# Moving the start columns of operand buffers for TensorE in a two-layer encoder trunk

## The chip, the cores and the metric

The kernel runs on one core of a Trainium2 chip. The metric is the device time of one execution in microseconds (us); of several executions the median counts. TensorE does the matrix products, ScalarE (ACT in the profile) and VectorE (DVE) prepare operands and drain results, and the queues of SyncE (SP) and GpSimd (POOL) issue most DMA transfers.

A matmul on TensorE has two operands in the on-chip memory. The **stationary** one, 128x128, is loaded into the array by an instruction of its own (LDWEIGHTS, row PEld of the profile). The **moving** one, here 256, 272 or 512 columns wide, streams past it (MATMUL, row PE). A float32 column is 4 bytes in each of the 128 partitions. "Column" below always means a place of 4 bytes along a partition.

## The reference

Two layers over 512 tokens of width 1024. Each is a token mixer and a gated feed-forward block, both with RMSNorm and a residual. What the change touches are two products: the `v` part of the second layer's mixer, and the second layer's last down projection.

```python
def gla_mixer(h, w_g2, b_g, norm_g):          # layer 1; h = rmsnorm(x) @ gla_w_in
    q, k, v, r, gl = jnp.split(h, [...], axis=-1)
    g = jax.nn.log_sigmoid((gl @ w_g2 + b_g).astype(f32)) / GLA_TAU
    ...                                        # chunked gated linear attention over q, k, v, g
    return o                                   # normed, times silu(r)

def conv_ffn(h, w_up, conv_w, conv_b, w_down):
    u, v = jnp.split(h @ w_up, 2, axis=-1)
    u = causal_dwconv(u, conv_w, conv_b)
    return (jax.nn.gelu(u, approximate=False) * v) @ w_down

for l in range(2):
    x = x + mixer(rmsnorm(x, mix_norm[l]))     # layer 0: pooling and short convolution; layer 1: GLA
    x = x + conv_ffn(rmsnorm(x, ffn_norm[l]), ...)
return rmsnorm(x, final_norm)
```

## The kernel before

Every product is done in three passes: each float32 operand is split into a high part (a copy rounded to the type float32r, made by ACT) and a low part (the rest, made by DVE), and high x high, high x low and low x high are added up in one accumulator. So each block of weights that DMA brings into a `raw` buffer is turned into a `hi` and a `lo` buffer before TensorE may use it: `high()` and `low()` inside `fetch_steps` (L260 and L264) for plain blocks, L531 and L537 inside `seven_weights` for the large products, which are done as seven half-size products (L650).

**Who is stationary.** In all large products the weights are stationary, in blocks of 128 columns, and activations move. In the `v` product it is the other way round: `v_chunk` (L1535 to L1537) has 128 tokens of `xh` or `xl` stationary and lets 256 or 272 columns of the weights `hi` or `lo` move. `v` has four column groups (272, 256, 256, 256 wide; the first holds 16 columns for the low-rank gate) and 8 rows of 128 in depth. A buffer takes 3, 3 and 2 depth rows of the wide group, or 4 and 4 of a narrow one. For each depth row and each of four token tiles there are three matmuls, so a buffer gives 36, 36, 24, or 48 matmuls: 96 with 272 columns and 288 with 256.

**Where operands begin.** The `hi` and `lo` buffers are 1088 columns long (`WPITCH`), which is 17 times 64, and hold up to 1024. Weights of the seven-product form begin 19 columns in (`SKEW`), those of `v` 48 columns in (`VG_SKEW`), those of plain blocks at 0. The last down tile is done in halves of 256 tokens. Its two weight blocks are used twice, so they are kept in two buffers of their own (`kept_block` in `last_pair`, L1028), which hold the 5 high blocks and 3 of the 5 low ones, from column 0; the other two low blocks go to a plain slot called `rest`. Per half and block there are 15 matmuls, 13 with a stationary operand in `kept` and 2 in `rest`: 60 in all.

The addresses in the built program show that the stationary tiles `xh` and `xl`, all activation slots and all weight buffers begin at the same place of a period of 64 columns. For a matmul, the column at which its moving operand begins less the one at which its stationary operand begins, modulo 64, is thus set by these offsets alone:

| matmuls | before | after |
|---|---|---|
| seven-product form (activation at 0, weights 19 in) | 45 | 45 |
| `v`, 256 wide (weights 48 in, then every 256) | 48 | 45 |
| `v`, 272 wide (depth rows 1, 2, 3 of a buffer) | 48, 0, 16 | 45, 45, 45 |
| last down tile, `kept` | 0 | 45 |
| last down tile, `rest` | 0 | 0 |

**What sets the order.** A planner in the kernel gives each step a due time (`at`, `then`, `block`), sorts the steps, and writes each engine's program in that order (`run_plan`). In the `v` stage each buffer's load, high and low step stand some 13, 8 and 6.6 us of planned time ahead of its use (`next_block`). Each finished column group is drained by ACT (`v_out`, L1542) and DVE (`v_low`, L1552). The first attention pair follows it. `seven_weights` also loads a tile `s31` from the pool's tag `sum`, the same tag as the kept buffers in the stage `dn`.

Of the kernel before, what the change touches and what calls it, by code (L numbers as in the profile page):

```python
# [7 lines left out]
F32 = mybir.dt.float32  # L8
F32R = mybir.dt.float32r
# [5 lines left out]
P = 128  # L15
# [16 lines left out]
WBLK = 1024  # L32
WPITCH = WBLK + 64
SKEW = 19
VG_SKEW = 48
NBIG = 48
NSIDE = 8
AHEAD = 1
# [74 lines left out]
def trunk_kernel(ctx, tc, xT, cols, w_first, w_lead, w_ab, w_pool, w_abo, w_abp, w_vg, w_qk, w_r, w_g2, w_go, w_up, w_dn, w_ds, w_de, out):  # L113
# [6 lines left out]
    wsp = ctx.enter_context(tc.tile_pool(name="wsp", bufs=4))  # L120
# [4 lines left out]
    def slot(dt=F32, name="s"):  # L125
        return big.tile([P, T], dt, tag="s", name=name)

    stage = {}
# [84 lines left out]
    def f32(ap):  # L213
        return ap.bitcast(F32)
# [5 lines left out]
    def down_blocks():  # L220
        yield from ((j, k0, kt) for k0, kt in zip(DOWN_AT, DOWN_K) for j in range(4))
        yield from ((j, k0, kt) for j in range(4, KD) for k0, kt in zip(DOWN_AT, DOWN_K))

    def weight_order():
        for j in range(4):
            for b in (4 + j, 8 + j, j):
                yield w_ab[b], KD, P
        for j in ABO:
            if not isinstance(j, tuple):
                yield w_abo[j], KD, P  # L230
        for l in range(2):
            for j, k0, kt in down_blocks():
                yield w_dn[l, j, :, k0 * P : (k0 + kt) * P], kt, P, SKEW * (l == 1 and j == KD - 1)
            if l == 0:
                off = 0
                for n, ks in zip(VG_COLS, VG_K):
                    for kt in ks:
                        yield w_vg[:, off : off + kt * n], kt, n, VG_SKEW
                        off += kt * n
                for j in TILE_ORDER:  # L240
                    yield w_go[j], KD, P
# [3 lines left out]
    ready = []  # L245
# [3 lines left out]
    def fetch_steps():  # L249
        src, kt, n, *skew = next(order)  # L250
        fetched[0] += 1
        m = kt * n
        h0 = skew[0] if skew else 0
        raw = wp.tile([P, WBLK], F32, tag="raw", name="raw")[:, :m]
        loads.append(nc.sync.dma_start(raw, src).ins)
        parts = []

        def high():
            parts.append(wsp.tile([P, WPITCH], F32R, tag="hi", name="hi")[:, h0 : h0 + m])
            S.activation(parts[0], raw, AF.Copy)  # L260

        def low():
            parts.append(wsp.tile([P, WPITCH], F32R, tag="lo", name="lo")[:, h0 : h0 + m])
            V.tensor_tensor(parts[1], raw, f32(parts[0]), ALU.subtract)  # L264
            ready.append([t.rearrange("p (k n) -> p k n", k=kt) for t in parts])

        return high, low

# [208 lines left out]
    def at(t, fn):  # L477
        events.append((t, len(events), fn))
# [24 lines left out]
    def seven_weights(src, base, pool, sums, behind=False, lead=None, later=0.0, begin=(26.0, 20.0, 15.4, 9.7), early=0.0, low31=None, times=None):  # L503
        w = {}

        def load_sum():
            s31 = w["s31"] = stage[pool].tile([P, WBLK], F32, tag="sum", name="s31", bufs=sums)
            part = src[:, None, D : D + QUARTER].broadcast_to([P, 2, QUARTER])
            nc.sync.dma_start(s31.rearrange("p (a n) -> p a n", a=2), part)

        def add_sum():
            part = src.rearrange("p (a n) -> p a n", a=4)[:, 0:4:3, :]
            G.dma_start(w["s31"].rearrange("p (a n) -> p a n", a=2), part, accum_op=ALU.add)  # L513

        def load_left():
            w["raw", 0] = wp.tile([P, WBLK], F32, tag="raw", name="raw")
            nc.sync.dma_start(w["raw", 0], src[:, :D])

        def load_right():
            w["raw", 1] = wp.tile([P, WBLK], F32, tag="raw", name="raw")  # L520
            nc.sync.dma_start(w["raw", 1][:, QUARTER:], src[:, D + QUARTER :])

        def tiles(kind, wide):
            if wide:
                return wsp.tile([P, WPITCH], F32R, tag=kind, name=kind)[:, SKEW : SKEW + WBLK]
            tag, bufs = "s" + kind[0], 2 if pool == "up" else 1
            return stage[pool].tile([P, T + 64], F32R, tag=tag, name=tag, bufs=bufs)[:, SKEW : SKEW + T]

        def high(name, src, wide=True):
            h = tiles("hi", wide)  # L530
            S.activation(h, src(), AF.Copy)  # L531
            w[name] = (h, src)

        def low(name, wide=True):
            h, src = w[name]
            lo = tiles("lo", wide)
            V.tensor_tensor(lo, src(), f32(h), ALU.subtract)  # L537
            w[name] = (h, lo)

        def s2_sum():  # L540
            s2 = w["raw", 1][:, :QUARTER]
            V.scalar_tensor_tensor(  # L542
                s2, w["s31"][:, QUARTER:], -1.0, w["raw", 0][:, :QUARTER], ALU.mult, ALU.subtract
            )

        def s4_sum():
            s2 = w["raw", 1][:, :QUARTER]
            V.tensor_tensor(s2, w["raw", 0][:, QUARTER:], s2, ALU.subtract)

        def queued_sum():  # L550
            with tc.issue_after(loads[-1]):
                load_sum()

        at(base - begin[0], queued_sum if behind else load_sum)
        at(base - begin[1], add_sum)
        steps = (
            (lambda: high("a1", lambda: w["raw", 0])), (lambda: low("a1")), (lambda: high("s31p", lambda: w["s31"])),
            s2_sum, (lambda: high("s2", lambda: w["raw", 1][:, :QUARTER], False)), (lambda: low("s2", False)),
            s4_sum, (lambda: high("a2", lambda: w["raw", 1])), (lambda: low("s31p")), (lambda: low("a2")),
        )  # L560
        when = (-6.75, -4.35, -2.7, -2.4, -1.65, -0.95, -0.3, 1.55, 1.5, 3.3)
        if pool == "up":
            when = (*when[:7], *((2.2, 1.5, 4.4) if lead is not None else (0.4, 1.5, 3.3)))
        if pool == "dn":
            when = (-4.2, -2.9, 0.0, -4.0, -2.2, -1.0, -0.3, 4.3, 0.9, 7.2)
        if pool == "gla":
            when = GLA_WHEN
        when = times or when
        if low31 is not None:
            when = (*when[:8], low31, when[9])  # L570
        if lead is not None and lead < 2:
            when = UP_FIRST[lead]
        at(base - (18.0 if lead == 0 else begin[2]), load_left)
        at(base - (13.0 if lead == 0 else begin[3]), load_right)
        for n, (t, step) in enumerate(zip(when, steps)):
            at(base + t + ((0, 0, 1.2, 1.2, 0.6, 0.6)[lead or 0] if 3 <= n <= 6 else later if n == 0 else 0.0) - (early if n < 7 else 0.0), step)

        return w
# [200 lines left out]
    def ffn(l, acc, mixed, finish, ahead, halves_last=False):  # L779
# [215 lines left out]
        def last_pair(p, base):  # L995
# [19 lines left out]
            def kept_block(n):  # L1015

                parts, side = [], P * (DOWN_K[0] - 2)

                def load():
                    src, kt, wide, _ = next(order)  # L1020
                    fetched[0] += 1
                    parts.append(wp.tile([P, WBLK], F32, tag="raw", name="raw")[:, : kt * wide])
                    loads.append(nc.sync.dma_start(parts[0], src).ins)

                def high():
                    if not rest:
                        rest.append(slot(F32R, "rest"))
                    parts.append(stage["dn"].tile([P, WBLK], F32R, tag="sum", name="kept", bufs=2))  # L1028
                    S.activation(parts[1][:, : 5 * P], parts[0], AF.Copy)

                def low():
                    raw, h = parts
                    more = rest[0][:, 2 * n * P : 2 * n * P + 2 * P]
                    V.tensor_tensor(h[:, 5 * P :], raw[:, :side], f32(h[:, :side]), ALU.subtract)
                    V.tensor_tensor(more, raw[:, side:], f32(h[:, side : 5 * P]), ALU.subtract)
                    blocks = h.rearrange("p (k n) -> p k n", n=P), more.rearrange("p (k n) -> p k n", n=P)
                    late[DOWN_AT[n]] = blocks[0][:, :5, :], [blocks[0][:, 5 + k, :] if k < 3 else blocks[1][:, k - 3, :] for k in range(5)]

                return load, high, low
# [49 lines left out]
        t = base + 9 * UNIT  # L1089
        blocks = list(down_blocks())  # L1090
        parts = {}
# [53 lines left out]
    parts = {}  # L1145
# [27 lines left out]
    with tc.manual_schedule(engines=set(planned)):  # L1173
# [7 lines left out]
        for n in range(2, 5):  # L1181
            k = lead[n][1]
# [47 lines left out]
    pool = [{} for _ in WINDOWS]  # L1230
# [131 lines left out]
    t = t0 - tile_us  # L1362
    for n in range(12):
        j, name = n // 3, ("pc", "px", "pb")[n % 3]
# [356 lines left out]
    t = 0.0  # L1721
# [370 lines left out]
```

## Time and profile before

| | us |
|---|---|
| median of three executions | 988.26 |
| lowest, highest | 988.03, 989.71 |
| the profiled execution, its own time | 988.62 |
| its span (first to last instruction) | 986.9 |

TensorE was busy for 977.9 us of the span, weight loads for 930.6, DVE for 899.7, ACT for 640.3, and the granted TensorE clock is 0.9 of full or more in every slice of the page. The `v` matmuls run from 459.8 to 508.9 us of the span; the last down tile's kept weights are used from 965.2 to 978.0 us.

Two things help in reading the rows of the prediction. The busy time and mean of a matmul row count its way through the array, and matmuls overlap, so a mean of 276 ns is not what one costs: what one costs is the distance from its start to the next one's start. A stretch of the span that holds nothing but a known number of matmuls, divided by that number, gives it. And all times of the views are microseconds from the start of the span, unless ns is written.

### The profile page before, as it was taken

The numbers are of one execution on the slowest core, as the hardware profiler recorded it, in microseconds if no ns is written. First come the engines' busy times: TensorE is split into PE (matmuls) and PEld (weight loads), VectorE is DVE, ScalarE is ACT, GpSimd is POOL, SyncE is SP. The second block draws the span as 40 slices with busy tenths as digits, with TensorE's granted clock in tenths as the row PEclk, the third lists the DMA queues.
The fourth block names the chain that finished last, engine by engine and source line by source line (L and its number), as shares of the span: only waits on it lengthen the run. The fifth ranks groups of instructions, "written<-read, shape, count | busy, mean of one in ns | idle before, by whom it ended". The sixth has DMA issues, their size and how long they took to land.

```text
span 986.9 us, 18789 instructions
## 1 busy us (share of the span) xinstructions
PE 977.9 (99%) x7396; PEld 930.6 (94%) x7396; DVE 899.7 (91%) x1410; ACT 640.3 (65%) x1079; POOL 90.9 (9%) x113
## 2 busy tenths in 40 slices
PE   9999999999999999999999999999999999999997
PEld 7888989999999988999999999899999999988997
DVE  7798999999999999889989889789999999899886
ACT  6454767766766666446777786667676666656553
POOL 0001111111101000002000000110110101000000
PEclk9999999999999999999999999999999999999999
DMA  7227677787787464726426453858687777464622
GB/s 260 76 85 221 162 162 185 197 217 184 198 196 185 111 164 112 183 83 176 127 79 171 120 124 108 218 144 200 182 216 185 200 188 194 114 153 124 169 82 99
DMA packets 70329, 156.81 MB, mean 159 GB/s; under 512 B 5888, under 2 KB 9344, under 8 KB 70240
## 3 DMA queue, kind: packets, MB, share of 16 engines
q1 hardware_dynamic: 51104, 119.55, 37.5%
q0 software_dynamic: 18848, 35.66, 22.3%
q8 instruction: 58, 0.95, 0.4%
q10 hardware_dynamic: 288, 0.40, 0.1%
q14 instruction: 31, 0.25, 0.1%
HBM read 150.86 MB, written 2.10 MB: 155 GB/s over the span
## 4 chain that ended last, share of the span: by engine, by line
PE 96%; DVE 2%; ACT 1%; DMA 0%; issue 0%; DVEq 0%
PE stx L650 36%; PE styz L650 21%; PE dn L305 11%; PE go L305 4%; PE dn L650 3%; PE stz L650 3%; PE pu L1168 2%; PE pc L305 2%; PE pb L305 2%; PE px L305 2%; PE vg L1535 2%; PE vg L1537 2%; PE vg L1536 2%; PE abo L305 1%; PE o L1606 1%; PE stw L650 1%
## 5 line engine op out<-in xcount | busy, mean ns | idle before, releaser
L537 DVE TENSOR_TENSOR lo<-raw,hi 128x1024 fp32r<-128x1024 f32 x124 | 151.1, 1220 | 6.8 <-ACT hi L531 6.8
L531 ACT ACTIVATE hi<-raw 128x1024 fp32r<-128x1024 f32 x124 | 129.9, 1056 | 27.5 <-PE styz L650 11.4
L513 POOL DMA_DIRECT2D s<-in_w_up x44 | 53.3, 1211 | 395.3 <-DVE u L820 74.8
L537 DVE TENSOR_TENSOR lo<-s,hi 128x1024 fp32r<-128x1024 f32 x62 | 75.5, 1218 | 0.0
L402 DVE SCALAR_TENSOR_TENSOR cacc<-u,colt,cacc 128x511 f32<-128x511 f32 x96 | 71.4, 744 | 1.6 <-ACT cacc L399 1.6
L399 ACT ACTIVATE cacc<-u,colt 128x512 f32<-128x512 f32 x48 | 39.2, 817 | 44.7 <-DVE u L823 41.7
L531 ACT ACTIVATE hi<-s 128x1024 fp32r<-128x1024 f32 x62 | 65.5, 1056 | 2.7 <-issue 1.2
L264 DVE TENSOR_TENSOR lo<-raw,hi 128x1024 fp32r<-128x1024 f32 (+3 forms) x63 | 63.9, 1019 | 3.1 <-ACT hi L260 2.9
L650 PE MATMUL stx<-th,hi 128*128 128x256 f32 x416 | 64.3, 277 | 0.0
L650 PE MATMUL stx<-tl,hi 128*128 128x256 f32 x416 | 64.1, 276 | 0.0
L650 PE MATMUL stx<-th,lo 128*128 128x256 f32 x416 | 64.1, 276 | 0.0
L650 PE MATMUL styz<-xh,hi 128*128 128x256 f32 x400 | 62.2, 277 | 1.3 <-ACT xh L757 1.3
L650 PE MATMUL styz<-xh,lo 128*128 128x256 f32 x400 | 61.7, 276 | 0.0
L650 PE MATMUL styz<-xl,hi 128*128 128x256 f32 x400 | 61.7, 276 | 0.0
L260 ACT ACTIVATE hi<-raw 128x1024 fp32r<-128x1024 f32 (+3 forms) x63 | 55.5, 884 | 2.8 <-PE stx L650 1.3
L650 PEld LDWEIGHTS stx<-th,hi 128*128 128x128 f32 x416 | 54.9, 188 | 0.2 <-ACT n L1790 0.2
L650 PEld LDWEIGHTS stx<-tl,hi 128*128 128x128 f32 x416 | 54.9, 188 | 0.0
L650 PEld LDWEIGHTS stx<-th,lo 128*128 128x128 f32 x416 | 54.9, 188 | 0.0
L650 PEld LDWEIGHTS styz<-xh,hi 128*128 128x128 f32 x400 | 53.0, 188 | 1.5 <-ACT xh L757 1.5
L650 PEld LDWEIGHTS styz<-xh,lo 128*128 128x128 f32 x400 | 52.9, 188 | 0.0
L650 PEld LDWEIGHTS styz<-xl,hi 128*128 128x128 f32 x400 | 52.8, 188 | 0.0
L531 ACT ACTIVATE sh<-raw 128x512 fp32r<-128x512 f32 x62 | 39.2, 632 | 18.1 <-DVE raw L542 18.1
(459 smaller groups left out, 2725.5 us busy)
## 6 DMA issues: line engine op xcount, KB each, us to landing
s<-in_w_up SPq DMA_DIRECT2D x44, 512.0 KB, 6.7
s<-in_w_up POOLq DMA_DIRECT2D x44, 512.0 KB, 6.6
raw<-in_w_up SPq DMA_DIRECT2D x44, 512.0 KB, 6.2
raw<-in_w_up SPq DMA_DIRECT2D x44, 256.0 KB, 3.2
raw<-in_w_dn SPq DMA_DIRECT2D x32, 320.0 KB, 2.9
raw<-in_w_ab SPq DMA_DIRECT2D x12, 512.0 KB, 3.5
s<-in_w_ds SPq DMA_DIRECT2D x8, 512.0 KB, 5.9
s<-in_w_ds POOLq DMA_DIRECT2D x8, 512.0 KB, 7.6
```

The lines of the kernel that those rows point to most:

```text
L260: S.activation(parts[0], raw, AF.Copy)
L264: V.tensor_tensor(parts[1], raw, f32(parts[0]), ALU.subtract)
L305: PE.matmul(out, w[k] if isinstance(w, list) else w[:, k, :], a[k], start=first and i == 0 and k == 0, stop=last and i == 2 and k == n - 1 ...
L399: S.activation(acc[0], u, AF.Identity, bias=col(bname, j), scale=col(wname, 2 * nj + j))
L402: V.scalar_tensor_tensor(a, u[:, : T - i], col(wname, (2 - i) * nj + j), a, ALU.mult, ALU.add)
L513: G.dma_start(w["s31"].rearrange("p (a n) -> p a n", a=2), part, accum_op=ALU.add)
L531: S.activation(h, src(), AF.Copy)
L537: V.tensor_tensor(lo, src(), f32(h), ALU.subtract)
L650: PE.matmul(b[out][:, ts], wt[k], a[k], start=first and i == 0 and k == 0, stop=i == 2 and k == len(a) - 1, skip_group_check=True,)
L1168: PE.matmul(pus[g], parts[k][w][:, g * P : (g + 1) * P], a[k], start=k == 0 and i == 0, stop=k == KD - 1 and i == 2,)
L1535: PE.matmul(o[c][:, :n], xh[kk][:, cs], h[:, k, :], start=kk == 0, stop=False)
L1536: PE.matmul(o[c][:, :n], xl[kk][:, cs], h[:, k, :], start=False, stop=False)
```

## The change

Three places change, and with them no arithmetic.

1. The weights of `v` begin 45 columns into their buffers instead of 48.
2. The depth rows of the 272-wide group lie 320 columns apart in the buffer instead of 272 (320 is 5 times 64). The raw buffer stays packed, so the three high and three low conversions of that group become two-dimensional (3 or 2 runs of 272 columns instead of one run of 816 or 544).
3. The kept weights of the last down tile begin 19 columns into their buffers; the tag `sum` of the stage `dn` has longer buffers for that (1088 columns instead of 1024), for `s31` too.

The order of the instructions on every engine is the same as before. Six instructions have another shape, the conversions of point 2.

```diff
-VG_SKEW = 48
+VG_SKEW = 45
+VG_PITCH = 320
@@ weight_order
-                        yield w_vg[:, off : off + kt * n], kt, n, VG_SKEW
+                        yield w_vg[:, off : off + kt * n], kt, n, VG_SKEW, VG_PITCH if n > 256 else n
@@ fetch_steps
         h0 = skew[0] if skew else 0
+        pitch = skew[1] if len(skew) > 1 else n
         raw = wp.tile([P, WBLK], F32, tag="raw", name="raw")[:, :m]
         loads.append(nc.sync.dma_start(raw, src).ins)
+        if pitch > n:
+            raw = raw.rearrange("p (k n) -> p k n", k=kt)
         parts = []

+        def place(name):
+            t = wsp.tile([P, WPITCH], F32R, tag=name, name=name)[:, h0 : h0 + kt * pitch]
+            return t.rearrange("p (k n) -> p k n", k=kt)[:, :, :n] if pitch > n else t
+
         def high():
-            parts.append(wsp.tile([P, WPITCH], F32R, tag="hi", name="hi")[:, h0 : h0 + m])
+            parts.append(place("hi"))
             S.activation(parts[0], raw, AF.Copy)

         def low():
-            parts.append(wsp.tile([P, WPITCH], F32R, tag="lo", name="lo")[:, h0 : h0 + m])
+            parts.append(place("lo"))
             V.tensor_tensor(parts[1], raw, f32(parts[0]), ALU.subtract)
-            ready.append([t.rearrange("p (k n) -> p k n", k=kt) for t in parts])
+            ready.append(parts if pitch > n else [t.rearrange("p (k n) -> p k n", k=kt) for t in parts])
@@ seven_weights, load_sum
-            s31 = w["s31"] = stage[pool].tile([P, WBLK], F32, tag="sum", name="s31", bufs=sums)
+            s31 = w["s31"] = stage[pool].tile([P, WPITCH if pool == "dn" else WBLK], F32, tag="sum", name="s31", bufs=sums)[:, :WBLK]
@@ last_pair, kept_block
-                    parts.append(stage["dn"].tile([P, WBLK], F32R, tag="sum", name="kept", bufs=2))
+                    parts.append(stage["dn"].tile([P, WPITCH], F32R, tag="sum", name="kept", bufs=2)[:, SKEW : SKEW + WBLK])
```

## The prediction

> **What bounds the kernel now.** I read the busy shares first, then the chain of work that ended last, then what TensorE waits for.
>
> ```profile
> span 986.9 us, 18789 instructions
> PE 977.9 (99%) x7396; PEld 930.6 (94%) x7396; DVE 899.7 (91%) x1410; ACT 640.3 (65%) x1079; POOL 90.9 (9%) x113
> PE 96%; DVE 2%; ACT 1%; DMA 0%; issue 0%; DVEq 0%
> PE styz L650 <- ACT xh L757: 1.3, 1, 1.3
> PE warm L200 <- DVE half L206: 1.1, 1, 1.1
> PE pu L1168 <- ACT xh L1162: 0.6, 1, 0.6
> PE vg L1535 <- DVE z L1477: 0.2, 1, 0.2
> ```
>
> 96% of the chain is TensorE, and its four waits (the last four rows) add up to 3.2 us, 0.2 of them in the `v` stage. So TensorE's own pace sets the end, and a nanosecond more or less per matmul is paid in full, as long as its operands keep arriving ahead of it. DVE at 91% is what could fall behind.
>
> The next view is the chain near the end, merged: start, length, what, how many matmuls. It holds two kinds of 256-wide matmuls side by side. (`dn` L305 there is the kept part, 13 of 15 with a stationary operand in `kept`.)
>
> ```profile
> 957.19 2.04 PE dn L650 x18
> 959.23 2.04 PE stx L650 x18
> 961.27 2.04 PE stz L650 x18
> 963.31 2.04 PE stx L650 x18
> 965.35 1.80 PE dn L305 x15
> 969.24 1.80 PE dn L305 x15
> 975.05 3.00 PE dn L305 x25
> ```
>
> The seven-product form takes 2.04/18 = 113.3 ns a matmul, the kept part 1.80/15 and 3.00/25 = 120.0 ns. Both are 256 columns wide, both in float32r. What differs is where the operands begin: moving less stationary start is 45 columns modulo 64 in the first, 0 in the second. The first kind is the kernel's bulk and keeps its pace elsewhere too, right behind the `v` stage for one:
>
> ```profile
> 510.68 1.36 PE styz L650 x12
> 512.04 1.36 PE stx L650 x12
> 513.40 1.36 PE stz L650 x12
> ```
>
> 1.36/12 is again 113.3 ns. Now the `v` stage by its weight buffers (stretch, its length, TensorE's busy time; the count includes matmuls still under way at the start). By the code they hold 36+36, 24, then six times 48 matmuls; in rows two to five the buffer's first matmul stands behind a gap and is left out, so 23, 47, 47 and 47 remain.
>
> ```profile
> 459.80:468.81 9.01, 9.01 (x72) 1.00 0.97 256
> 469.83:472.70 2.87, 2.87 (x24) 1.00 1.07 315
> 473.71:479.06 5.35, 5.35 (x48) 1.00 0.38 112
> 479.62:484.95 5.33, 5.33 (x48) 1.00 0.25 68
> 486.42:491.95 5.53, 5.53 (x49) 1.00 0.29 92
> 491.95:497.61 5.66, 5.66 (x51) 1.00 0.16 45
> 497.61:503.26 5.65, 5.65 (x51) 1.00 0.09 19
> 503.26:508.92 5.66, 5.66 (x50) 1.00 0.21 77
> ```
>
> Per matmul: 9.01/72 = 125.1 and 2.87/23 = 124.8 ns for the 272-wide ones; then 113.8 and 113.4 ns for the first two narrow buffers, and 117.7, 117.9, 117.7 and 117.9 ns for the other four. The clock is 1.00 in every row. The pace of 113.3 ns for 256 columns makes 113.3 x 272/256 = 120.4 ns for 272 (an estimate, no row has 272 columns at another start). So the wide ones run 4.4 to 4.7 ns over it, four narrow buffers 4.5, two narrow buffers hardly at all.
>
> **The change part by part.**
>
> *Wide buffers of `v` (45 columns in, 320 apart).* All 96 go from 48, 0 and 16 to 45, the value of the bulk. If that value is what counts, each falls to 120.4: 72 x 4.7 = 0.34 us and 24 x 4.4 = 0.11 us, 0.45 us together.
>
> *Narrow buffers (48 to 45).* 192 x 4.5 = 0.86 us from the last four, and 47 x 0.5 = 0.02 us from the first: 0.88 us.
>
> *Kept blocks (0 to 45).* 52 of the 60 matmuls gain 120.0 - 113.3 = 6.7 ns, 0.35 us; the 8 with `rest` keep theirs.
>
> Sum: 0.45 + 0.88 + 0.35 = 1.68 us, an upper end, since 113.3 is the best pace that any row shows.
>
> The bounds. By the addresses in the built program no matmul of this kernel so far has a **moving** operand that begins off a multiple of 16 columns; the 45 of the bulk comes from weights that stand still. From above, nothing shows a pace under 113.3. From below, the worst row is the kept one, 6.7 ns over the bulk: were that the price of an odd start on each of the 384, `v` would lose 384 x 6.7 = 2.57 us against its best, and 2.57 - 1.33 = 1.24 us against now. I take the bulk's pace for both roles, as the kept rows and the bulk differ in nothing but that difference, and keep the 1.24 us of loss (with the kept blocks' gain 988.26 + 1.24 - 0.35 = 989.15 us) for the range.
>
> The Trainium skill (TensorE: Matmul & The Clock Gate, section Step-by-step: what each phase is for) says that TensorE has two independent read ports, and that loading the next weights takes no bandwidth from the running matmul. By that rule where the two begin would be worth nothing and the sum would be 0. The trace does not agree: 113.3 against 120.0 ns within three microseconds, at 963.31 and 965.35.
>
> *Conversions of the wide group.* Three on ACT and three on DVE become 2 or 3 runs of 272. No row has such a write of float32r. Bounds: nothing, or at worst as much again (1.00 us for the DVE one).
>
> ```profile
> 456.84 0.87 ACT L260 ACTIVATE hi<-raw 128x816 fp32r<-128x816 f32 x1
> 457.67 1.00 DVE L264 TENSOR_TENSOR lo<-raw,hi 128x816 fp32r<-128x816 f32 x1
> 459.79 0.29 PE L1535 MATMUL vg<-hi,xh 128*128 128x272 f32 x1
> 522.67 0.35 DVE L1566 TENSOR_TENSOR k<-k,ek 128x192 f32<-128x192 f32 x1
> 525.55 0.42 DVE L1793 TENSOR_TENSOR q<-stz,q 128x256 f32<-128x256 f32 x1
> ```
>
> The nearest row in runs, the attention's `k` (3 runs of 64), takes 0.35 us for 192 columns, against 0.42 for 256 in one run: about the same for its size, so I take nothing. The first low part is the closest: it ends at 458.67, its first user, the third matmul of `v`, starts two steps of 0.12 us behind the first, at 460.03, so 1.3 us cover it.
>
> *Longer buffers in the stage `dn`.* 64 columns each; no instruction changes by it, cost nothing.
>
> **Does anything eat the gain on the way?** Three places.
>
> First, the gate logits, where TensorE waits for a bank.
>
> ```profile
> 469.79 0.16 DVE L341 TENSOR_SCALAR v<-ss 128x4 f32<-128x4 f32 x1 [0.41 <-PE ss L383]
> 485.38 2.73 DVE L1477 TENSOR_SCALAR z<-z,colt 128x512 f32<-128x512 f32 x4 [0.18 <-PE z L1475]
> ```
>
> DVE had 0.18 us to spare when TensorE's logits came. TensorE will be 0.47 us earlier there (0.45 + 0.02). But DVE's work before it hangs, by way of the norm's sums at 469.79, on TensorE too, which has won the first 0.34 us by then. 0.34 + 0.18 is over 0.47, so nothing is lost.
>
> Second, the attention pairs behind the `v` stage, where low parts come late.
>
> ```profile
> 510.72 0.39 ACT L1790 ACTIVATE q<-stx 128x256 f32<-128x256 f32 x1 [1.06 <-PE stx L650]
> 514.25 2.36 DVE L537 TENSOR_TENSOR lo<-raw,hi 128x1024 fp32r<-128x1024 f32 x2 [0.85 <-ACT hi L531]
> 523.20 2.43 DVE L537 TENSOR_TENSOR lo<-raw,hi 128x1024 fp32r<-128x1024 f32 x2
> 526.47 0.62 PE L650 MATMUL styz<-xh,lo 128*128 128x256 f32 x4
> ```
>
> A low part ends at 525.63 and is used at 526.47: 0.84 us to spare. TensorE comes 1.33 us earlier. DVE stood idle for 0.85 us at 514 for ACT, which in turn had waited 1.06 us for the pair's first product of TensorE (first row), so DVE moves up by 0.85 at least, and by 0.47 more as it is earlier since the logits: 1.32 us in all. Even by the 0.85 alone 0.84 - (1.33 - 0.85) = 0.36 us stay. Nothing is lost, but it is the step I trust least; if the cover were gone, up to 0.5 us of the 1.33 would be.
>
> Third, the end.
>
> ```profile
> 975.31 1.88 DVE L1948 TENSOR_TENSOR xall<-xall,bc 128x512 f32<-128x512 f32 x3
> 978.08 0.43 DVE L980 TENSOR_TENSOR dn<-dn,rs 128x256 f32<-128x256 f32 x1 [0.90 <-PE dn L305]
> ```
>
> DVE's scaling ends at 977.19, and it waits 0.90 us for the last kept matmul; half of 0.35 us is won by TensorE in that stretch. The rest of the end (square, sums, root, output) starts from that matmul and moves up with it.
>
> **The sum.** The profiled execution took 988.62 us, 1.7 more than its span; less 1.68 it is 986.94. It lies 0.36 over the median of the three runs, 988.26, from which I forecast 988.26 - 1.68 = **986.6 us**.
>
> **The rivals.**
>
> *Time, not place, in `v`.* The first two narrow buffers ran at 113.4 to 113.8 ns with the very same starts as the four at 117.8; between them lies only the gap of the logits at 485. So the phase between loads and matmuls in time has a part in it, and at 45 the `v` matmuls may fall in either. Then `v` keeps its time and the kept blocks alone gain: 988.26 - 0.35 = 987.9 us. Against it: the bulk restarts behind many gaps, and its pace in the rows above is 113.3 each time.
>
> *An odd start costs a little.* Each of the 384 moving runs may touch one unit of memory more than before. At a quarter of the kept block's 6.7 ns, 1.7 ns each, that is 0.65 us, leaving 1.03: 987.2 us. Nothing in the trace speaks for or against it. A page of the Trainium skill is near it (SBUF — State Buffer, section Specifications (TRN2)): lines of 16 bytes, with a penalty at each crossing to a new one. 45 columns are 180 bytes, a quarter line past a boundary; no run here shows such a crossing of a moving operand.
>
> *An odd start costs more than it cures (slower).* Place: all 384 `v` matmuls. If being off a 16-column boundary makes the moving read slower by the kept blocks' 6.7 ns and the present 4.5 ns remain, `v` loses 2.57 us, and with 0.35 won the time is 988.26 + 2.22 = 990.5 us. It ends slower from 0.35/384 = 0.9 ns per matmul on, when nothing is cured. For it: no moving operand here was ever tried there. Against: weight loads that begin 19 columns in (first row) are not slower than those of `xh` at 0 (second).
>
> ```profile
> L650 PEld LDWEIGHTS stx<-th,hi 128*128 128x128 f32 x416 | 54.9, 188 | 0.2 <-ACT n L1790 0.2
> L1537 PEld LDWEIGHTS vg<-lo,xh 128*128 128x128 f32 x128 | 24.3, 190 | 0.0
> ```
>
> *Nothing moves.* The pace belongs to something other than the places, or the freed time goes into waits for DVE everywhere: 988.3 us. Against it stand the rows of the end, where both paces lie side by side. (It is also what the TensorE page's rule above gives.)
>
> **How the numbers follow.** Full gain (986.6) 0.63; time, not place (987.9) 0.15; a little for odd starts (987.2) 0.08; slower (990.5) 0.09; nothing (988.3) 0.05. The range from 985.8 to 989.2 us goes down 0.8 us under the forecast, half the spread of the runs shown (988.03 to 989.71), and up to the lower bound worked out above; it leaves out the slower case and the tails. A difference of 0.2%, about 2.0 us, is what a measurement of this kernel can tell from no change; the forecast gain is 0.17%. For faster by more than that, the time must be under 986.28, 0.3 us below the forecast: about a quarter of the full-gain case by the spread of the runs shown, 0.17. Slower by more: the slower case, 0.09. Within: 0.74.
>
> **What would show it.** In the profile of the changed kernel: the last four narrow buffers at 5.43 to 5.45 us for 48 matmuls instead of 5.66; 72 wide ones in 8.67 us instead of 9.01; kept rows of 15 in about 1.71 us instead of 1.80; the first product behind `v` at about 507.9 instead of 509.2; no new wait of TensorE between 509 and 530. I am wrong if the narrow rows stay at 117 or rise over it, if the kept rows stay at 120, or if these fall and the span does not.

## The result and the profile after

| | before | after |
|---|---|---|
| median of 17 executions, us | 988.41 | 990.48 |
| lowest, highest | 988.02, 989.94 | 989.62, 992.99 |
| profiled execution, its own time | 988.62 | 990.26 |
| its span | 986.9 | 988.6 |

The changed kernel is slower: the ratio is 1.0019, with a 95% interval from 1.0012 to 1.0026, that is 1.2 to 2.6 us. 986.6 us was forecast. The head of the page of the changed kernel (lines have moved by 8: L1535 is L1543 now, L650 is L658, L305 is L313):

```profile
span 988.6 us, 18789 instructions
PE 979.7 (99%) x7396; PEld 932.2 (94%) x7396; DVE 899.9 (91%) x1410; ACT 640.0 (65%) x1079; POOL 91.4 (9%) x113
PE 96%; DVE 2%; ACT 1%; DMA 0%; issue 0%; DVEq 0%
```

TensorE bounds it as before. It is busy for 1.8 us more, with the same instructions. The stretches of the `v` buffers, cut as in the prediction (36 and 36 wide matmuls, 23 wide, three times 47 narrow, three times 48 narrow):

```profile
460.27:464.92 4.65, 4.64 (x36) 1.00 1.00 321
464.92:469.57 4.65, 4.65 (x38) 1.00 1.01 192
470.59:473.57 2.98, 2.98 (x24) 1.00 1.07 319
474.57:480.22 5.65, 5.65 (x48) 1.00 0.36 108
480.78:486.44 5.66, 5.66 (x48) 1.00 0.32 90
487.91:493.55 5.64, 5.64 (x48) 1.00 0.21 73
493.55:499.31 5.76, 5.76 (x50) 1.00 0.14 46
499.31:505.07 5.76, 5.76 (x50) 1.00 0.18 58
505.07:510.83 5.76, 5.76 (x50) 1.00 0.10 36
```

Every narrow buffer runs at 120.0 to 120.4 ns a matmul (5.76/48, 5.66/47), where 113.3 were forecast and 113.4 to 117.9 stood before. Once settled, single starts lie 117 and 123 ns apart in turn in five of the six, 116 and 124 in the second; the mean is 120.0 in all. The wide ones take 4.65/36 = 129.2 and 2.98/23 = 129.6 ns, after 125. The stage from its first matmul to the end of its last stretch takes 510.83 - 460.27 = 50.56 us; before it was 508.92 - 459.80 = 49.12. So `v` lost **1.44 us**.

The kept part gained. In the chain near the end, one row of the seven-product form and two of the kept part (L313):

```profile
965.19 2.04 PE stx L658 x18
967.23 1.71 PE dn L313 x15
971.12 1.71 PE dn L313 x15
```

1.71 instead of 1.80 us for 15, as forecast. Over the whole end TensorE won 0.2 us by it: starts of the same matmuls lie 1.89 us later than before ahead of the kept part and 1.69 later behind it.

The two stages make 1.44 - 0.2 = 1.24 us. The rest of the 1.7 us between the two spans, some 0.5 us, arises in the first 7 us, on work that is the same in both, so it is not the change's. The first matmuls of the kernel before:

```profile
5.24 1.19 PE L1168 MATMUL pu<-xh,hi_lead 128*128 128x512 f32 x4 [0.65 <-ACT xh L1162]
6.28 1.08 PE L1168 MATMUL pu<-xh,lo_lead 128*128 128x512 f32 x4
```

and of the changed one:

```profile
5.37 1.61 PE L1176 MATMUL pu<-xh,hi_lead 128*128 128x512 f32 x4 [0.46 <-ACT xh L1170]
6.81 1.07 PE L1176 MATMUL pu<-xh,lo_lead 128*128 128x512 f32 x4
```

The first four matmuls start 0.13 us later and take 1.44 us after 1.04. The profiles below that leave this work alone are 0.05 to 1.0 us behind the profile of the kernel before after their first 16 us, with or without the changed parts. For what an edit does, the length of its own stage is therefore the better measure than the span.

### The profile page after: what moved, and what is told of

Read it like the earlier page. It is cut to its first block, busy times and chain, and to the rows that moved or that the text cites. A ratio compares the mean times of both kernels' runs of the same rounds, so it can differ in the third digit from the quotient of the medians.

```text
span 988.6 us, 18789 instructions
## 1 busy us (share of the span) xinstructions
PE 979.7 (99%) x7396; PEld 932.2 (94%) x7396; DVE 899.9 (91%) x1410; ACT 640.0 (65%) x1079; POOL 91.4 (9%) x113
## 4 chain that ended last, share of the span: by engine, by line
PE 96%; DVE 2%; ACT 1%; DMA 0%; issue 0%; DVEq 0%
PE stx L658 36%; PE styz L658 21%; PE dn L313 11%; PE go L313 4%; PE dn L658 3%; PE stz L658 3%; PE pu L1176 2%; PE pc L313 2%; PE pb L313 2%; PE px L313 2%; PE vg L1543 2%; PE vg L1545 2%; PE vg L1544 2%; PE abo L313 1%; PE o L1614 1%; PE stw L658 1%
## 5 line engine op out<-in xcount | busy, mean ns | idle before, releaser
L658 PE MATMUL stx<-th,hi 128*128 128x256 f32 x416 | 64.3, 277 | 0.0
L658 PE MATMUL stx<-th,lo 128*128 128x256 f32 x416 | 64.1, 276 | 0.0
L658 PE MATMUL stx<-tl,hi 128*128 128x256 f32 x416 | 64.1, 276 | 0.0
L658 PE MATMUL styz<-xh,hi 128*128 128x256 f32 x400 | 62.2, 277 | 1.3 <-ACT xh L765 1.3
L658 PE MATMUL styz<-xh,lo 128*128 128x256 f32 x400 | 61.7, 276 | 0.0
L658 PE MATMUL styz<-xl,hi 128*128 128x256 f32 x400 | 61.7, 276 | 0.0
L658 PEld LDWEIGHTS stx<-th,hi 128*128 128x128 f32 x416 | 54.9, 188 | 0.2 <-ACT n L1798 0.2
L658 PEld LDWEIGHTS stx<-tl,hi 128*128 128x128 f32 x416 | 54.9, 188 | 0.0
L658 PEld LDWEIGHTS stx<-th,lo 128*128 128x128 f32 x416 | 54.9, 188 | 0.0
L658 PEld LDWEIGHTS styz<-xh,hi 128*128 128x128 f32 x400 | 53.0, 188 | 1.5 <-ACT xh L765 1.5
L658 PEld LDWEIGHTS styz<-xh,lo 128*128 128x128 f32 x400 | 52.8, 188 | 0.0
L658 PEld LDWEIGHTS styz<-xl,hi 128*128 128x128 f32 x400 | 52.8, 188 | 0.0
```

The lines of the kernel that those rows point to most:

```text
L658: PE.matmul(b[out][:, ts], wt[k], a[k], start=first and i == 0 and k == 0, stop=i == 2 and k == len(a) - 1, skip_group_check=True,)
```

## The experiments

In the profiles a stage's length is read to some 0.02 us; a ratio of two times is uncertain by 0.1%, 1 us. So each place was judged by the pace of the matmuls, and the times are given beside it.

### One part alone, and another place for all of `v`

All diffs are against the changed kernel, or the version named. `kept_only` leaves out the change's first two parts (lines stand one further than in the changed kernel, in `x19` three):

```diff
-VG_SKEW = 45
-VG_PITCH = 320
+VG_AT = (48, 48, 48, 48, 48, 48, 48, 48, 48)
+VG_PITCH = 272
@@ weight_order
+                starts_at = iter(VG_AT)
                 for n, ks in zip(VG_COLS, VG_K):
                     for kt in ks:
-                        yield w_vg[:, off : off + kt * n], kt, n, VG_SKEW, VG_PITCH if n > 256 else n
+                        yield w_vg[:, off : off + kt * n], kt, n, next(starts_at), VG_PITCH if n > 256 else n
```

> The change's third part alone: v's weights lie as before (48 columns in, wide rows 272 apart), the kept blocks of the last down tile begin 19 columns in. Every theory that lets the kept rows gain their 0.35 us (15 matmuls in 1.71 us instead of 1.80) gives 0.35 us under the kernel before, ratio 0.9996. If the longer buffers in that stage cost something of their own, it shows here as a ratio over 1.

988.48 us against 988.83 before: ratio 0.9994 (0.9983 to 1.0005). The kept rows of 15 take 1.71 us, so this part gains its 0.2 to 0.3 us, too little for a ratio of times to show. The profile holds something else, the narrow buffers of `v` at their old place 48:

```profile
474.54:479.89 5.35, 5.35 (x48) 1.00 0.40 113
480.45:485.99 5.54, 5.54 (x48) 1.00 0.29 81
487.45:492.79 5.34, 5.34 (x48) 1.00 0.25 93
503.67:509.11 5.44, 5.44 (x50) 1.00 0.28 95
```

Their paces are 113.8, 117.9, 113.6 and 113.3 ns. In the profile of the kernel before the first two buffers ran at 113 and the last four at 118. Here it is the second alone that runs at 118, with the same places. So 48 has **two** paces; in the profiles with 48, which of them a stretch falls into is settled anew behind each gap of TensorE, differs from profile to profile, and then holds until the next gap.

`v19` puts all nine buffers of the changed kernel to 19:

```diff
-VG_SKEW = 45
+VG_AT = (19, 19, 19, 19, 19, 19, 19, 19, 19)
```

> All nine buffers of v begin 19 columns in instead of 45, wide rows 320 apart, kept blocks as in the change. Theory SUM (stationary and moving start add up, as if the weight load read its block from the far end, so that 19 + 0 is the bulk's 0 + 19): 113.3 ns for 256 columns and 120.4 for 272, v ends at about 507.6 us, the kernel 1.7 us under the one before (ratio 0.998). Theory ODD (a moving run that begins off a multiple of 4 or 16 columns is slow by itself): 19 is as odd as 45, so 120 ns and 128 ns as in the changed kernel, 2 us over the one before (ratio 1.002). Theory DIFFERENCE (moving less stationary start, 45 good) has 19 as an untried value and gives nothing better than 113.3.

989.24 us, ratio 1.0003 (0.9994 to 1.0013). Two of its rows:

```profile
460.69:465.24 4.55, 4.55 (x37) 1.00 0.93 321
504.41:510.01 5.60, 5.60 (x50) 1.00 0.22 83
```

116.7 ns narrow, in all six buffers, and 126.4 wide: neither the 113.3 of SUM nor the 120 of ODD. 19 is as odd as 45 and better. Both theories fall in the form they were stated in.

### Single places

Since each buffer can have its own place, one execution shows six. These five versions, one execution each (989.37 to 990.47 us), differ only in the list:

```diff
+VG_AT = (48, 48, 48, 44, 46, 36, 40, 47, 13)     # mix1
+VG_AT = (16, 16, 16, 0, 32, 16, 24, 51, 64)      # mix2
+VG_AT = (32, 32, 32, 52, 56, 60, 4, 8, 20)       # mix3
+VG_AT = (51, 51, 51, 28, 61, 3, 35, 49, 2)       # mix4
+VG_AT = (28, 28, 28, 30, 26, 12, 27, 29, 28)     # mix5
```

> A look at single buffers of v: the three wide ones 48 columns in with rows 320 apart, the six narrow ones at 44, 46, 36, 40, 47 and 13. ODD with a unit of 16 columns: all six near 120 ns. ODD with a unit of 4: 44, 36 and 40 at 113 to 118, the others near 120. ODD with a unit of 2: 46 is good too. SUM: the nearer to 19 the better, so 13 before the rest. DIFFERENCE: 44, 46 and 47 next to 45 as slow as that (120). The wide ones: if the pitch alone helps, under the 125 ns of before.

> The same with the wide ones at 16 and the narrow ones at 0, 32, 16, 24, 51 and 64. SUM: 16 and 24 near 113, 0 and 64 at the kept blocks' old 120, 51 bad. ODD with a unit of 4 or 16: all but 51 under 120. A theory in which place does not count at all and only the restart behind a gap does: no order by place, 0 and 64 may differ.

> More places with the stationary tiles at 0: wide at 32, narrow at 52, 56, 60, 4, 8 and 20. If the place within 16 columns orders them (3 and 4: 116.7; 8 and over: 118.8 to 120), 52, 4 and 20 give 116.7, 56 and 8 about 119 and 60 120. If the difference modulo 64 orders them, they follow their neighbours: 52 as 51 (116.7), 20 as 19 (116.7), 4 and 60 as 0 (120).

> More places: wide at 51, narrow at 28, 61, 3, 35, 49 and 2. Place within 16 columns: 3, 35, 49 and 2 give 116.7 or less, 28 and 61 119 to 120. Difference modulo 64: 3, 2 and 61 as 0 (120), 35 as 36 (116.7), 49 as 48 (113.3 or 117.8), 28 as 24 (120). A place that gives 113.3 would be the one to use for all.

> Places around 28: wide at 28, narrow at 30, 26, 12, 27, 29 and 28. If 28 is a good place by itself, the last buffer runs at 113.3 again, here without a gap ahead of it; if only the restart behind the gap did it, it stays at the pace of its neighbours (117 to 120). If place works in steps of 4 columns, 30, 26, 27 and 29 are near 117 to 120 though next to it.

Paces in ns a matmul of the narrow buffers, each a stretch divided by its 47 or 48 matmuls, the stationary operand at 0:

| place | pace | place | pace | place | pace | place | pace |
|---|---|---|---|---|---|---|---|
| 0 | 119.6 | 16 | 117.9 | 32 | 118.5 | 48 | 113.3 or 117.8 |
| 2 | 120.0 | 19 | 116.7 | 35 | 116.7 | 49 | 120.0 |
| 3 | 117.0 | 20 | 118.1 | 36 | 116.8 | 51 | 116.7 |
| 4 | 118.8 | 24 | 120.0 | 40 | 118.8 | 52 | 119.1 |
| 8 | 116.7 | 26 | 129.4 | 44 | 119.1 | 56 | 118.5 |
| 12 | 118.5 | 27 | 119.6 | 45 | 120.0 | 60 | 117.2 |
| 13 | 120.2 | 28 | 114.3 | 46 | 120.0 | 61 | 122.1 |
| | | 29, 30 | 121.5, 121.3 | 47 | 120.0 | 64 | 119.8 |

The four places 3, 19, 35 and 51 agree within 0.3 ns, 0 and 64 within 0.2. So place counts, and it is not the gap alone. ODD falls for every unit: 24 and 0 are as slow as 45, and 3, 19, 35 and 51 are faster. SUM falls too: 16 and 20, the nearest to 19, take 117.9 and 118.1, and 13 and 24 take 120.2 and 120.0. But the order is no simple rule either: 26, 28 and 30, two columns apart, give 129.4, 114.3 and 121.3, and 51 and 52, or 48 and 49, differ as well. Most places stand for one buffer of one execution, so a second pace, as 48 has it, is not ruled out for them. Two rows of `mix5`, for 26 and for 28 without a gap ahead of it:

```profile
480.08:486.16 6.08, 6.08 (x48) 1.00 0.30 86
504.76:510.28 5.52, 5.52 (x50) 1.00 0.11 42
```

28 starts at the pace of 29 ahead of it and settles at 113.3 within the buffer. The wide buffers, rows 320 apart, take 123.3 ns at 48 (4.44 us for 36), 126.7 at 16 and 32, and 125.0 at 51. At 28 the first two buffers take 126.4 and 126.9 and the third 123.5 (2.84 us for 23), so there are two paces there as well. At 48 with rows 272 apart it was 125.1. None reaches the 120.4 of my estimate.

### The same difference, made by the other operand

This is the run that bears on the step which failed. `x19` moves the tiles `xh` and `xl` 19 columns on instead, and lets two narrow buffers and the wide ones begin at 0 (or 64):

```diff
-    xh = [cp.tile([P, T], F32R, tag=f"xh{k}", name=f"xh{k}") for k in range(KD)]
-    xl = [cp.tile([P, T], F32R, tag=f"xl{k}", name=f"xl{k}") for k in range(KD)]
+    xhl = cp.tile([P, 2 * KD * T + 64], F32R, tag="xhl", name="xhl")
+    xh = [xhl[:, XAT + k * T : XAT + k * T + T] for k in range(KD)]
+    xl = [xhl[:, XAT + (KD + k) * T : XAT + (KD + k) * T + T] for k in range(KD)]
+XAT = 19
+VG_AT = (0, 0, 0, 0, 19, 38, 3, 48, 64)          # x19
+XAT = 16
+VG_AT = (16, 16, 16, 61, 16, 0, 35, 32, 48)      # x16
```

> All xh and xl tiles are moved 19 columns on, so that in v the stationary operand begins at 19. v's wide buffers begin at 0, the narrow ones at 0, 19, 38, 3, 48 and 64. The seven-product matmuls with xh or xl moving then have both operands at 19 (they are slower or not on purpose; the time of the whole says nothing). Theory DIFFERENCE WITH AN EVEN STREAM (what counts is the moving start less the stationary one, 45 good, but the stream itself wants to begin at a multiple of 16): 0 and 64 run at 113.3 ns, the wide ones at 120.4, 19 at 120; the xh products near 120. Theory V IS OTHER (v never reaches the bulk's pace at that difference, whatever the streams' starts): 0 and 64 stay at 117 to 120. Theory PLACE OF THE STREAM ALONE: 0 and 64 at 120 as they did with the stationary tiles at 0, 19 at 116.7, 48 at 113.3 or 117.8.

The first wide buffer, the narrow one at 0 (47 matmuls, its first left out) and the last four narrow ones (38, 3, 48 and 64):

```profile
469.66:474.11 4.45, 4.45 (x37) 1.00 0.90 254
484.35:489.70 5.35, 5.35 (x48) 1.00 0.17 31
498.47:504.21 5.74, 5.74 (x49) 1.00 0.28 91
504.21:509.81 5.60, 5.60 (x50) 1.00 0.14 46
509.81:515.57 5.76, 5.76 (x51) 1.00 0.11 27
515.57:521.03 5.46, 5.46 (x50) 1.00 0.20 72
```

64 runs at 5.46/48 = 113.8 ns, the bulk's pace but for its first few matmuls, straight behind a buffer at 48 that ran at 120.0. The one at 0, behind a gap, takes 5.35/47 = 113.8 ns and settles at 113, 113, 114. With the stationary operand at 0 the same 64 took 119.8 and the same 0 took 119.6. Both have the difference 45 and a moving operand on the 64-column grid on which all buffers begin; the changed kernel's `v` has the same 45 with a moving operand off that grid, and takes 120.0. DIFFERENCE WITH AN EVEN STREAM is what fits the narrow buffers; V IS OTHER and PLACE OF THE STREAM ALONE fall. The wide buffers at 0 run at 123.6, not at 120.4: there the theory is 3 ns off.

The products in which `xh` or `xl` moves change with it. The first row is 12 of them (both operands at 19, difference 0), the second 12 with other activations at 0 against weights at 19; the third, from another part of the kernel, 24 matmuls 512 wide with `xh` and `xl` moving at 19 and the weights at 0:

```profile
306.27 1.44 PE styz L661 x12
307.71 1.37 PE stx L661 x12
34.48 5.60 PE px L316 x24
```

120.0, 114.2 and 233.3 ns. In the kernel before the last took 5.44 us:

```profile
33.28 5.44 PE px L305 x24
```

or 226.7 ns, with both operands at 0. So 512-wide matmuls lose 6.6 ns as well; in `x16`, with `xh` and `xl` at 16, the same 24 take 5.60 us again. Here the moving start and the difference change together, and which of the two it is was not separated. The whole of `x19` took 1008.72 us and of `x16` 1003.84 us, which says nothing of `v`, as all products with `xh` or `xl` moving are changed in them.

> The same with xh and xl moved 16 columns on, so that pairs of v can be tried with both operands moved by 16: narrow buffers at 61 (45 + 16), 16 (0 + 16), 0, 35 (19 + 16), 32 and 48, wide ones at 16. If only the difference and the place within 16 columns count, 61 repeats 45's 120.0 with its alternating 117 and 123, 16 repeats 0's 120, 35 repeats 19's 116.7; 0 (difference 48) runs at 113.3 or 117.8 and 32 as 16 did (117.8). If the absolute place counts, they fall elsewhere.

With the stationary tiles at 16, 0 (difference 48) took 113.8, 16 took 120.0, 32 took 117.7 and 35 took 116.7 ns: as 48, 0, 16 and 19 did with them at 0. 48 gave 118.5, as 32 had. But 61, whose difference is 45, settled at 123 where 45 had given 120.0: off the grid it is slow there too. So among places on multiples of 16 the difference orders the paces, and off them it does not always.

### Back to 48, and a better place

`v48p` is the changed kernel with its 45 put back; `v28` uses the place that was best for the narrow buffers:

```diff
-VG_SKEW = 45
+VG_AT = (48, 48, 48, 48, 48, 48, 48, 48, 48)     # v48p
+VG_AT = (48, 48, 48, 28, 28, 28, 28, 28, 28)     # v28
```

> The change with 45 put back to 48 and the rest left: rows of the wide buffers 320 apart, kept blocks at 19. If the harm sits in the 45 alone, the wide rows take 123.4 instead of 125.2 ns (96 x 1.8 = 0.17 us), the kept ones gain 0.2 to 0.3 us, the narrow ones run at 113.3 or 117.8 behind each gap as before: 0.4 us under the kernel before give or take 0.6 (ratio 0.9996). If pitch or kept blocks harm by themselves, it is over 1.

> A version made from the looks: v's narrow buffers all at 28 (113.5 ns in the look at 28), its wide ones at 48 with rows 320 apart (123.3 ns there), kept blocks at 19. If 28 is a place where the stream always settles at 113.3, v takes 288 x 113.5 + 96 x 123.4 ns plus 0.4 us for the starts behind gaps = 44.9 us against 47.3 in the changed kernel and 45.9 in the profile before; with the kept blocks' 0.2 to 0.3 us the kernel ends 1.2 to 1.3 us under the one before (ratio 0.9987) and 2.6 under the changed one. If 28 was luck behind one gap, as 48 is, some buffers stand at 117 to 120 and the ratio is near 1.

`v48p`: 988.76 us, ratio 0.9999 (0.9990 to 1.0008). The loss is gone, so it sits in the 45; no harm of pitch and kept blocks shows. The pitch makes the wide matmuls faster, 4.44 us for 36 after 4.51. Of its narrow buffers two ran at 117.8 and four at 113.3.

`v28`: 987.89 us against 988.81, ratio 0.9986 (0.9977 to 0.9995), by this measurement faster than the kernel before. Its rows from the fourth to the last buffer but one:

```profile
474.30:479.67 5.37, 5.37 (x48) 1.00 0.27 67
480.23:485.58 5.35, 5.35 (x48) 1.00 0.18 31
487.50:492.86 5.36, 5.36 (x49) 1.00 0.28 96
492.86:498.30 5.44, 5.44 (x51) 1.00 0.14 38
498.30:503.73 5.43, 5.43 (x50) 1.00 0.03 10
```

All at 113.1 to 114.3 ns, behind each gap. But the gap ahead of 487.50 is longer, as the waits of TensorE say:

```profile
PE vg L1544 <- DVE z L1486: 0.6, 1, 0.6
```

It was 0.2 us before. `v28z` moves the one DVE step that stands ahead of the logits:

```diff
-                next_block()
+                next_block(low=5.0 if (b, i) == (2, 1) else 6.6)
```

> v28 with one step moved: DVE drains the four gate logits before it makes the low part of the third column group's second buffer, not after (due 5.0 instead of 6.6 us ahead of that buffer's use, which has some 7 us to spare). In v28 TensorE waited 0.6 us there for DVE, which had no idle time ahead of the logits; in the kernel before it waited 0.2. Theory GIVEN BACK (0.4 to 0.5 us of what 28 wins goes into that wait because DVE is late): the wait falls to 0.2 us or less, the time to 0.4 to 0.6 us under v28 (some 987.4 us, ratio 0.998 to the kernel before). Theory NOISE OF ONE PROFILE (the 0.6 us was a single execution's): no change against v28 (0.9986). In both the paces of the v matmuls stay at 113.3 and 123.3 ns.

DVE's draining of the logits in `v28`, and in `v28z`:

```profile
486.47 2.73 DVE L1486 TENSOR_SCALAR z<-z,colt 128x512 f32<-128x512 f32 x4
```

```profile
486.21 2.73 DVE L1486 TENSOR_SCALAR z<-z,colt 128x512 f32<-128x512 f32 x4 [1.35 <-PE z L1484]
```

Now DVE waits for TensorE, and TensorE's wait is gone from its list. The `v` stage takes 508.93 - 460.74 = 48.19 us, against 509.18 - 460.55 = 48.63 in `v28`. But this does not show GIVEN BACK. The two profiles differ 19 us ahead of the logits, too, where ACT waits for a load and DVE for ACT. The high part concerned, in `v28` and in `v28z`:

```profile
467.21 1.06 ACT L269 ACTIVATE hi<-raw 128x1024 fp32r<-128x1024 f32 x1 [1.64 <-DMA raw<-in_w_vg]
```

```profile
466.09 1.06 ACT L269 ACTIVATE hi<-raw 128x1024 fp32r<-128x1024 f32 x1 [0.34 <-DMA raw<-in_w_vg]
```

The load came 1.3 us later in `v28`, and DVE was late from there on. With the load of `v28z` the moved low part, 1.22 us long, would have fitted into the 1.35 us for which DVE now stands idle. So NOISE OF ONE PROFILE explains the 0.4 us as well. Nor does the time show a gain over `v28`: 988.52 us against 988.87, ratio 0.9998 (0.9989 to 1.0007), on another chip than `v28`. What moving the step is worth is not shown.

Nor do the times settle what 28 is worth: of two versions with the same places, `v28` is faster than the kernel before and `v28z` the same. The profiles show that all 12 narrow buffers at 28 in these two reach 113.3. But the stage of `v28` is no shorter than that of `v48p` and `kept_only` (48.50 and 48.48 us), where 48 fell into its better pace for four and five of the six buffers.

The stage's length in all of them, from the stretches:

| | before | after | kept_only | v19 | v48p | v28 | v28z |
|---|---|---|---|---|---|---|---|
| `v`, us | 49.12 | 50.56 | 48.48 | 49.32 | 48.50 | 48.63 | 48.19 |
| ratio of times to before | 1 | 1.0019 | 0.9994 | 1.0003 | 0.9999 | 0.9986 | 0.9998 |

## Why the prediction was wrong

**What bounds the kernel: right.** 1.44 us more in `v` and 0.2 less in the end went straight into TensorE's busy time and the span; no new wait of TensorE arose in the changed kernel.

**Kept blocks: the pace right, the gain too large.** 1.71 us for 15 was forecast and measured, and the eight with `rest` stay at some 120 as forecast. The 60 matmuls win 0.3 us, and the end as a whole 0.2 instead of 0.35: the 18 of the seven-product form behind the first 15 take 2.18 us where they took 2.09.

**Narrow and wide buffers of `v`: wrong.** The step that failed is "I take the bulk's pace for both roles". The reason given for it, that the kept rows and the bulk differ in nothing but the difference, does not carry it: they differ in where the stationary operand begins, and in both the moving one begins at the same place. I read a rule in the difference of the two starts out of rows in which the moving operand always lay on the grid, and used it for a case in which it does not. `x19` has shown that the difference 45 is good for `v`, too, as long as the stationary operand carries the offset: 113.8 ns at 0 and at 64. With the moving one carrying it, it is 120.0. Why the role matters stays open. (That being off the grid is always a loss is not shown: 28 settles at 113.3.) Instead of 1.33 us won, 1.44 were lost.

**The rival "An odd start costs more than it cures" has the direction, and its time, 990.5, is the measured one by luck.** Its price per matmul was too high: 384 x 6.7 = 2.57 us, while `v` lost 1.44, or 3.8 a matmul. What the stages of the two profiles explain is 1.44 - 0.2 = 1.24 us, the lower end of the interval of 1.2 to 2.6. Why the medians lie further apart is not shown, as the other executions have no profile; it would follow if the `v` of the kernel before often falls into the better pace of 48. In the profile of `kept_only` that `v`, with the same places, was shorter by 0.64 us; measured from it the change costs 1.44 + 0.64 - 0.2 = 1.9 us. Its reason was wrong as well: being off a 16-column boundary is not by itself what costs, as 19 and 35 run at 116.7, faster than 0 and 24, and 28 settles at 113.3. Nor is it the lines of 16 bytes, 4 columns, that the Trainium skill gives (SBUF — State Buffer, section Specifications (TRN2)): 24 begins on such a line and runs at 120.0, 19 and 35 do not and run at 116.7. "An odd start costs a little" falls with it, since `v` lost.

**"Time, not place, in `v`" was half right.** At 48 the restart behind a gap does choose between 113.3 and 117.8, as `kept_only` shows with its other choice. At 45 there was nothing to choose: six buffers out of six settle at 120.0.

**"Nothing moves" falls.** Moving only where the stationary operand begins took `v` at 64 from 119.8 to 113.8 ns. The rule of the Trainium skill that stands beside that rival (TensorE: Matmul & The Clock Gate, section Step-by-step: what each phase is for), that loading weights takes nothing from the running matmul, does not give this: here the pace of 256-wide float32r matmuls depends on where the weights begin.

**The estimate of 120.4 for 272 columns was too low.** The best that any run showed is 123.3, at 48 with rows 320 apart, and at 0 with the stationary operand at 19.

**Conversions: right.** Taken at nothing extra, and the DVE one measures 1004 ns after 1002:

```profile
L272 DVE TENSOR_TENSOR lo<-raw,hi 128x816 fp32r<-128x816 f32 x2 | 2.0, 1004 | 0.0
```

**What eats the gain on the way.** With a gain that never came this was not tried by the change itself. In `v28` TensorE did wait 0.4 us more at the first of the three places, the logits, but the late load of that profile is enough to explain it. At the second, the attention pairs, TensorE waited in no run, but in none was `v` as much shorter as the 1.33 us of the forecast.

## What to carry to other kernels

A pace that is tied to a difference of two addresses in the trace is known for the arrangement in which it was seen, here with the offset on the stationary operand. Before using it the other way round, ask whether any row has the roles swapped; where none has, that is the cost to bound most widely, and one execution with a different place per buffer answers it. When a stage may settle into one of two paces, compare the stage's stretches in several profiles, not spans.

## What the runs showed that was not expected

- Matmuls that follow each other without a gap settle into a fixed pattern of starts, most within some ten of them: 113, 113, 114 ns; or 117, 118, 118; or 117 and 123 in turn. The pattern goes with the places of the two operands, and 48 has two of them.
- A shift of the moving operand by 2 columns changes the pace of 256-wide matmuls between 114.3 and 129.4 ns (28 and 26). Why 28 is good is open: no rule in the difference or in the place within 16 columns that was tried gives both 28 and its neighbours.
- 512-wide matmuls take twice the bulk's 113.3 ns with both operands at 0 (226.7 ns), and 6.6 ns more when the moving one begins 16 or 19 columns in.
- The same first four large matmuls took 1.04 us (the kernel before), 1.44 us (the changed one) and 1.87 us (`v28z`), in executions that do the same work up to there.
